# Small transfers and recurrent states begun on GpSimd's queue, and the delta sample states updated by one fp32r pass

## The chip, the cores and the metric

The kernel runs on one core of a Trainium2 chip. The metric is the device time of one execution in microseconds; lower is better. The engines are TensorE (PE, with its weight loads PEld), VectorE (DVE), ScalarE (ACT), GpSimd (POOL) and SyncE (SP, which here only issues DMAs). "SPq", "ACTq" and "POOLq" in a row are the queues of these engines: issuing a DMA is an instruction there. Sixteen DMA engines move the data.

## The reference

Two layers of a recurrent decoder run for 256 prompt tokens and 8 x 4 sample tokens (288 columns in all) with shared weights, width 2048. Cut to what matters here:

```python
# layer 0: delta-rule heads and an RG-LRU; layer 1: mLSTM heads
for layer in range(2):
    mix = delta_lru_mixer(x, ...) if layer == 0 else mlstm_mixer(x, ...)
    h = layer_norm(ALPHA * x + mix)
    h = layer_norm(ALPHA * h + square(relu(h @ w_up)) @ w_down)
    x = h + sigmoid(h @ w_ple_gate) * (p[layer] @ w_ple)

# the gated delta rule, chunk by chunk (one chunk of 4 tokens for a sample)
v_new = u_i - w_i @ s
o     = (q_i * exp(g_i)) @ s + qk_i @ v_new
s     = s * exp(g_last) + (k_i * exp(g_last - g_i)).T @ v_new     # state, 128 x 128 per head
```

The last line is done for 8 samples and 8 heads: 64 states of 128 x 128. The outputs are x and every state (conv, delta, lru, mlstm c, n, m).

## The kernel before, in words

The work of TensorE is nearly all weight products. A weight slab of 512 KB (`raw`) is loaded on SP (`convert`, L394), split by ScalarE into a high part `hi` (L294) and by VectorE into a low part `lo` (L295), and multiplied in three fp32r passes with the split activations `ah`/`al` (`tiles`, L416, 128x288 moving). Up to three slabs are prepared ahead, with four buffers.

Everything else is written as side work: Python generators (`delta_gates`, `delta_head`, `delta_sample`, `lru_block`, `mlstm_gates`, `mlstm_head`, `mlstm_sample`) that `tick` advances by one `yield` after some twelve weight matmuls. A scheduler turns the program into one instruction list for each engine, in which every instruction waits for its inputs; nothing overtakes on an engine or in its queue. DMAs that move states and small tiles are instructions in these lists too. The side matmuls have the line of the helper `mm` (L268); transposes are L272, VectorE's helpers are L255, L258 and L262, ScalarE's is L265.

The places that the change touches:

- `delta_gates` computes the gates of all heads on 8 partitions, writes them to DRAM (`dgc`, `dds`), and reloads them broadcast or regrouped (`gcb` for each head in `delta_head`, `rs`). These run on ScalarE's queue, `gcb` on SP's.
- `conv` loads the previous rows of a channel block (`sconv` into `cin`) and stores the new ones (`out_conv`) on SP.
- `delta_sample` has 8 heads by 2 groups of 4 samples (g). It loads each group of states `S` (256 KB; four buffers) for the products `m<-S,win`, with windows that GpSimd copies (L1019), solves for `y` (tile `sy`), and then loads every `S` once more for the update. For the update `y4` places the four samples of a group beside each other (128x512, zeros elsewhere), `kh` masks the keys of one head, and `m<-y,kh` is one plain fp32 matmul of 128x512 for each head and group, 16 in all. VectorE adds it to the decayed state, which SP stores.
- `mlstm_gates` does for layer 1 what `delta_gates` does for layer 0 (`mds`, `mrs`, `dw`, `w`, `dsc`, `scB`, `dng`) on ScalarE's queue; `mlstm_head` loads `ngb`, `mlstm_sample` loads and stores 16 states `cn` on SP.

```python
            y4 = lp.tile([128, 4, 128], F32, name="y4", bufs=1)
            self.tt(y4, y[:, g:g + 1].to_broadcast([128, 4, 128]),
                    c[:, C_B4:C_B4 + 4][:, :, None].to_broadcast([128, 4, 128]), ALU.mult)
```

Of the kernel before, what the change touches and what calls it, by code (L numbers as in the profile page):

```python
# [8 lines left out]
F32 = mybir.dt.float32  # L9
# [24 lines left out]
C_H8 = C_B4 + 4  # L34
C_B8 = C_H8 + 8
# [10 lines left out]
def const_table():  # L46
# [11 lines left out]
    c[:, C_B4:C_B4 + 4] = (r[:, None] // 32 == np.arange(4)[None])  # L58
    c[:, C_H8:C_H8 + 8] = ((r[:, None] % 32) // 4 == np.arange(8)[None])
# [159 lines left out]
class Trunk:  # L219
# [299 lines left out]
    def scratch(self, layer):  # L519
# [7 lines left out]
        self.nc.sync.dma_start(raw, self.t["p"][layer])  # L527
# [139 lines left out]
    def conv(self, lp, acc, c):  # L667
# [4 lines left out]
        nc.sync.dma_start(x[:, S0:], self.t["sconv"][c])  # L672
# [3 lines left out]
        nc.sync.dma_start(self.t["conv"][c], x[:, NP:])  # L676
# [20 lines left out]
    def delta_gates(self, acc, lp, T):  # L697
# [5 lines left out]
        nc.scalar.dma_start(rst, self.t["rows"][:, 0])  # L703
# [13 lines left out]
        nc.scalar.dma_start(self.dgc, gc)  # L717
# [135 lines left out]
    def delta_head(self, lp, h, kq, v, z, out):  # L853
# [3 lines left out]
        nc.sync.dma_start(gcb, self.dgc[h:h + 1].to_broadcast([128, NT]))  # L857
# [77 lines left out]
        nc.sync.dma_start(self.t["delta_p"][h], S[:, 1])  # L935
# [20 lines left out]
    def delta_sample(self, lp, win, out):  # L956
# [46 lines left out]
        X = res[0]  # L1003
        y, o = B("sy", bufs=1), B("oo")
# [3 lines left out]
        def load(h, g):  # L1008
            s = lp.tile([128, 4, 128], F32, name="S", bufs=4)
            nc.sync.dma_start(s, state(h, g))  # L1010
            return s

        for g in range(2):
# [16 lines left out]
            nc.scalar.copy(y[:, g], py)  # L1030
            yield
# [21 lines left out]
        for g in range(2):  # L1053
            y4 = lp.tile([128, 4, 128], F32, name="y4", bufs=1)
            self.tt(y4, y[:, g:g + 1].to_broadcast([128, 4, 128]),
                    c[:, C_B4:C_B4 + 4][:, :, None].to_broadcast([128, 4, 128]), ALU.mult)

            def keys(h):
                kh = lp.tile([128, 128], F32, name="kh", bufs=2)
                self.act(kh, ksc[:, g], AF.Copy, scale=c[:, C_H8 + h:C_H8 + h + 1])  # L1060
                return kh

            kh = keys(0)
            yield
            for h in range(8):
                s = load(h, g)
                pu = self.pm([128, 4, 128])
                self.mm(pu, kh, y4)
                if h < 7:
                    kh = keys(h + 1)  # L1070
                for b in range(4):
                    self.stt(s[:, b], s[:, b], self.eglS[:, h, 4 * g + b:4 * g + b + 1], pu[:, b],
                             ALU.mult, ALU.add)
                nc.sync.dma_start(self.t["delta_s"][h, :, 4 * g:4 * g + 4], s)
                yield
# [31 lines left out]
    def lru_block(self, lp, n, xr, gates, out):  # L1107
# [3 lines left out]
        nc.sync.dma_start(w, self.t["wri"][n])  # L1111
# [42 lines left out]
    def layer0_mixer(self, x, n_out):  # L1154
        nc, tc, t = self.nc, self.tc, self.t
        with ExitStack() as ctx:
# [50 lines left out]
            nc.sync.dma_start(t["lru"], self.hl)  # L1207
# [3 lines left out]
    def mlstm_gates(self, acc, lp, T):  # L1211
# [7 lines left out]
        nc.scalar.dma_start(rst, self.t["rows"][:, 1])  # L1219
        nc.scalar.dma_start(rmx, self.t["rows"][:, 2])  # L1220
# [20 lines left out]
        nc.scalar.dma_start(self.t["mm"], mo)  # L1241
        self.ts(ng, g, -1.0, ALU.mult)
        self.dng = self.dr.tile([8, NT], F32, name="dng")
        nc.scalar.dma_start(self.dng, ng)
# [8 lines left out]
        for n, r in enumerate((b4(a), mg, nm)):  # L1253
            nc.scalar.dma_start(ds[n].rearrange("b h t -> h b t"), r)
        self.rs = lp.tile([128, 3, 2], F32, name="mrs")
        for n in range(3):
            nc.scalar.dma_start(self.rs[:, n], ds[n].rearrange("(g b) h t -> (b h t) g", g=2))
        dw = self.dr.tile([8, 8, 4], F32, name="dw")
        nc.scalar.dma_start(dw, wr)
        self.w4 = lp.tile([128, 8], F32, name="w4")  # L1260
        for q in range(4):
            nc.scalar.dma_start(self.w4[32 * q:32 * q + 32], dw.rearrange("h b t -> (b t) h"))
# [3 lines left out]
        nc.scalar.dma_start(dsc, sc)  # L1266
# [285 lines left out]
```

## Time and profile before

| what | value |
|---|---|
| time, median of 3 runs | 2912.96 us (2909.19 to 2916.35) |
| profiled execution | 2916.8 us, its span 2915.0 us |
| granted clock of TensorE | 0.999 |
| TensorE busy | 2888.7 us, 99% |
| VectorE, ScalarE busy | 1732.1 us (59%), 1318.7 us (45%) |
| GpSimd busy | 57.9 us (2%), 197 instructions |
| DMA | 487.15 MB in 155298 packets, 167 GB/s in the mean |

The profile shows one execution. A time in a row is in microseconds from the start of the span; "[1.06 <-DMA S<-in_sdelta]" behind a row means that the engine was idle for 1.06 us before it and that the arrival of S ended this. The issuing of DMAs is not counted as busy time.

### The profile page before, as it was taken

The page shows a single profiled execution, that of the slowest core. Times are in us where ns is not written, and L with a number is a line of the kernel's source. Part 1 is how long each engine was busy: PE and PEld are TensorE (multiplying, and loading weights), DVE is VectorE, ACT ScalarE, POOL GpSimd, SP SyncE. Part 2 cuts the span into 40 slices and gives each one's busy share as a digit, 9 for nine tenths or more (in the row PEclk, how much of TensorE's full clock was granted, in tenths as well). Part 3 has the DMA queues.
Part 4 walks back from the last instruction along what each step waited for, and adds up shares of the span by engine and source line. Part 5 has one row for each costly group of instructions (what it writes and reads, how often), then busy time and mean ns, then how long its engine had stood idle before and what let it go on. Part 6 is the DMA issues. An engine that isn't in the chain of part 4 may idle for free.

```text
span 2915.0 us, 52851 instructions
## 1 busy us (share of the span) xinstructions
PE 2888.7 (99%) x21728; PEld 2839.1 (97%) x21728; DVE 1732.1 (59%) x2872; ACT 1318.7 (45%) x2171; POOL 57.9 (2%) x197
## 2 busy tenths in 40 slices
PE   8999999999999999999999999999999999999999
PEld 7999889999999999999999999999999999999999
DVE  7787787754454454455766666567445445445574
ACT  5555676543343343443634444436334334334362
POOL 1000100000000000000000000000000000000000
PEclk9999999999999999999999999999999999999999
DMA  6444475455555555555446665554555554555543
GB/s 225 134 127 128 151 233 174 134 191 166 167 164 164 165 167 166 162 165 166 159 157 201 198 201 172 184 167 159 166 163 163 167 167 162 165 166 166 165 156 132
DMA packets 155298, 487.15 MB, mean 167 GB/s; under 512 B 28552, under 2 KB 35888, under 8 KB 155056
## 3 DMA queue, kind: packets, MB, share of 16 engines
q1 hardware_dynamic: 151632, 483.68, 51.6%
q8 instruction: 170, 2.79, 0.4%
q10 hardware_dynamic: 3424, 0.10, 0.1%
q14 instruction: 72, 0.59, 0.1%
HBM read 466.12 MB, written 17.58 MB: 166 GB/s over the span
## 4 chain that ended last, share of the span: by engine, by line
PE 91%; DVE 5%; ACT 2%; DMA 1%; issue 1%; SPq 0%; ACTq 0%; DVEq 0%
PE acc L416 86%; PE m L268 4%; DVE Y L255 1%; DVE lo L295 1%; PE m L272 1%; ACT hi L294 1%; ACT junk L265 0%; PE m L470 0%; ACT L265 0%; DMA bh<-in_x 0%; DVE cv L258 0%; DVE al L255 0%; DVE mq L258 0%; DVE bl L255 0%; DMA S<-in_sdelta 0%
## 5 line engine op out<-in xcount | busy, mean ns | idle before, releaser
L295 DVE TENSOR_TENSOR lo<-raw,hi 128x1024 fp32r<-128x1024 f32 (+1 forms) x841 | 1027.1, 1223 | 680.6 <-ACT hi L294 679.6
L294 ACT CAST hi<-raw 128x1024 fp32r<-128x1024 f32 (+1 forms) x841 | 880.1, 1048 | 1007.3 <-PE acc L416 708.4
L416 PE MATMUL acc<-ah,hi 128*128 128x288 f32 x3328 | 998.9, 301 | 6.7 <-ACT hi L294 4.9
L416 PE MATMUL acc<-bh,hi 128*128 128x288 f32 x3328 | 989.6, 298 | 0.0
L416 PE MATMUL acc<-ah,lo 128*128 128x288 f32 x3328 | 985.1, 296 | 0.2 <-DVE lo L295 0.2
L416 PE MATMUL acc<-al,hi 128*128 128x288 f32 x3328 | 982.0, 297 | 0.9 <-DVE al L295 0.5
L416 PE MATMUL acc<-bh,lo 128*128 128x288 f32 x3328 | 981.3, 295 | 0.0
L416 PE MATMUL acc<-bl,hi 128*128 128x288 f32 x3328 | 974.1, 294 | 0.6 <-DVE bl L255 0.3
L416 PEld LDWEIGHTS acc<-ah,hi 128*128 128x128 f32 x3328 | 627.1, 189 | 12.6 <-ACT hi L294 4.9
L416 PEld LDWEIGHTS acc<-bh,hi 128*128 128x128 f32 x3328 | 624.0, 188 | 7.7 <-issue 7.1
L416 PEld LDWEIGHTS acc<-ah,lo 128*128 128x128 f32 x3328 | 627.7, 189 | 3.7 <-issue 2.3
L416 PEld LDWEIGHTS acc<-al,hi 128*128 128x128 f32 x3328 | 627.3, 189 | 3.6 <-issue 1.4
L416 PEld LDWEIGHTS acc<-bl,hi 128*128 128x128 f32 x3328 | 624.9, 188 | 1.8 <-DVE bl L255 0.8
L416 PEld LDWEIGHTS acc<-bh,lo 128*128 128x128 f32 x3328 | 625.2, 188 | 0.4
L265 ACT ACTIVATE tmp<-acc 128x288 f32<-128x288 f32 x160 | 65.8, 411 | 307.8 <-PE acc L416 307.7
L255 DVE TENSOR_TENSOR tmp<-tmp 128x288 f32<-128x288 f32 x128 | 58.8, 459 | 155.0 <-ACT tmp L265 155.0
L258 DVE SCALAR_TENSOR_TENSOR Y<-Y,acc 128x288 f32<-128x288 f32 x128 | 58.2, 455 | 112.0 <-PE acc L416 112.0
L258 DVE SCALAR_TENSOR_TENSOR cv<-cin,params,cv 128x312 f32<-128x312 f32 x96 | 51.5, 536 | 0.5
L258 DVE SCALAR_TENSOR_TENSOR cn<-cn,scB,m 128x257 f32<-128x257 f32 x64 | 27.9, 478 | 18.9 <-PE m L268 18.9
L265 ACT ACTIVATE Y<-Y,params 128x288 f32<-128x288 f32 x64 | 37.5, 633 | 0.3
L294 ACT CAST bh<-tmp 128x288 fp32r<-128x288 f32 x80 | 34.7, 434 | 6.2 <-DVE tmp L258 4.4
L258 DVE SCALAR_TENSOR_TENSOR tmp<-tmp,Z 128x288 f32<-128x288 f32 x32 | 14.6, 457 | 38.3 <-ACT tmp L265 38.3
(386 smaller groups left out, 1554.0 us busy)
## 6 DMA issues: line engine op xcount, KB each, us to landing
raw<-in_w_up SPq DMA_DIRECT2D x256, 512.0 KB
raw<-in_w_down SPq DMA_DIRECT2D x256, 512.0 KB
raw<-in_w_in_o SPq DMA_DIRECT2D x96, 512.0 KB
raw<-in_w_in_e SPq DMA_DIRECT2D x95, 512.0 KB
raw<-in_w_gate SPq DMA_DIRECT2D x64, 512.0 KB
raw<-in_w_out_e SPq DMA_DIRECT2D x32, 512.0 KB
raw<-in_w_out_o SPq DMA_DIRECT2D x32, 512.0 KB
cn<-in_smlstm SPq DMA_DIRECT2D x16, 514.0 KB
```

The lines of the kernel that those rows point to most:

```text
L255: return self.nc.vector.tensor_tensor(out=out, in0=a, in1=b, op=op)
L258: self.nc.vector.scalar_tensor_tensor(out=out, in0=a, scalar=s, in1=b, op0=op0, op1=op1)
L265: return self.nc.scalar.activation(out, a, f, **k)
L268: self.nc.tensor.matmul(out, l, r, start=start, stop=stop)
L272: self.nc.tensor.transpose(out, a, self.ident[:n, :n])
L294: self.nc.scalar.copy(hi, src)
L295: self.nc.vector.tensor_sub(lo, src, hi.bitcast(F32))
L416: self.nc.tensor.matmul(acc, l[:, k], x[r](8 * kb + k), start=at == 0, stop=at == n - 1)
```

## The change

First, nearly every DMA that isn't x, a parameter, a constant, a weight slab or the result y is issued by GpSimd (`nc.gpsimd`) and no more by SP or ScalarE. SP's instruction list goes from 1050 to 865 rows, GpSimd's from 172 to 415, and ScalarE issues no DMA any more.

Second, the keys (`ksc`) and `y` of `delta_sample` are split into a high and a low fp32r part (`parts_by_head`), each part is written to DRAM by head (`kd`, `yd`, 8 DMAs each), and reloaded so that the 128 partitions of a tile hold the four kinds of part products of two heads (4 DMAs into tiles named `kq`, 6 into tiles named `mq`). With them `m<-y,kh` is one fp32r matmul of one pass, which sums all part products; `y4` is made 8 times in place of 2. There are 16 such matmuls as before.

```diff
-        nc.sync.dma_start(x[:, S0:], self.t["sconv"][c])
+        nc.gpsimd.dma_start(x[:, S0:], self.t["sconv"][c])
...
-        nc.scalar.dma_start(self.dgc, gc)
+        nc.gpsimd.dma_start(self.dgc, gc)
...
-            nc.scalar.dma_start(self.rs[:, n], ds[n].rearrange("(g b) h t -> (b h t) g", g=2))
+            nc.gpsimd.dma_start(self.rs[:, n], ds[n].rearrange("(g b) h t -> (b h t) g", g=2))
...
-        nc.sync.dma_start(gcb, self.dgc[h:h + 1].to_broadcast([128, NT]))
+        nc.gpsimd.dma_start(gcb, self.dgc[h:h + 1].to_broadcast([128, NT]))
...
+        kd = self.parts_by_head(lp, "kd", ksc)
...
-            nc.sync.dma_start(s, state(h, g))
+            nc.gpsimd.dma_start(s, state(h, g))
...
+            if g == 1:
+                yd = self.parts_by_head(lp, "yd", y)
...
-        for g in range(2):
-            y4 = lp.tile([128, 4, 128], F32, name="y4", bufs=1)
...
-            for h in range(8):
-                s = load(h, g)
-                pu = self.pm([128, 4, 128])
-                self.mm(pu, kh, y4)
...
+        kg, yg = ([lp.tile([128, 2, 2, 128], F32, name=n) for _ in range(2)] for n in ("kq", "mq"))
+        for m in range(2):
+            for dst, src, parts in ((kg, kd, ((0, 0, 2), (64, 0, 2))), (yg, yd, ((0, 0, 1), (32, 0, 2), (96, 1, 1)))):
+                for at, first, n in parts:
+                    nc.gpsimd.dma_start(dst[m][at:at + 32 * n].rearrange("p n g d -> p n (g d)"),
+                                      src[2 * m:2 * m + 2, first:first + n].rearrange("n a b r d -> (a b r) n d"))
+        yield
+        yield
+        for m in range(4):
+            for g in range(2):
+                y4 = lp.tile([128, 4, 128], F32R, name="y4", bufs=1)
+                self.tt(y4, yg[m // 2][:, m % 2, g:g + 1].to_broadcast([128, 4, 128]),
+                        c[:, C_B4:C_B4 + 4][:, :, None].to_broadcast([128, 4, 128]), ALU.mult)
+                for i in range(2):
+                    h = 2 * m + i
+                    s = load(h, g)
+                    kh = lp.tile([128, 128], F32R, name="kh", bufs=2)
+                    self.act(kh, kg[m // 2][:, m % 2, g], AF.Copy, scale=c[:, C_H2 + i:C_H2 + i + 1])
+                    yield
+                    pu = self.pm([128, 4, 128])
+                    self.mm(pu, kh, y4)
...
+    def parts_by_head(self, lp, name, src):
+
+        dst = self.dr.tile([4, 2, 4, 8, 256], F32, name=name)
+        for n in range(2):
+            part = lp.tile([128, 2, 128], F32R, name="cm")
+            if n == 0:
+                self.nc.scalar.copy(part, src)
+                hi = part
+            else:
+                self.nc.vector.tensor_sub(part, src, hi.bitcast(F32))
+            for b in range(4):
+                self.nc.gpsimd.dma_start(dst[:, n, b],
+                                       part[32 * b:32 * b + 32].bitcast(F32).rearrange("p g d -> p (g d)"))
+        return dst
...
-            nc.scalar.dma_start(ds[n].rearrange("b h t -> h b t"), r)
+            nc.gpsimd.dma_start(ds[n].rearrange("b h t -> h b t"), r)
...
-        nc.sync.dma_start(ngb, self.dng[h:h + 1].to_broadcast([128, NT]))
+        nc.gpsimd.dma_start(ngb, self.dng[h:h + 1].to_broadcast([128, NT]))
...
-            nc.sync.dma_start(cn, self.t["smlstm"][h, :, gs])
+            nc.gpsimd.dma_start(cn, self.t["smlstm"][h, :, gs])
```

How the lists of the engines change at three places. At the start, SP's list of before has the small loads among the weight slabs of layer 0 (`raw<-in_w_in_e`):

```order
L394 DMA raw<-in_w_in_e 128x1024 x5
L672 DMA cin_140<-in_sconv 128x56
L394 DMA raw<-in_w_in_e 128x1024
L672 DMA cin_141<-in_sconv 128x56
L394 DMA raw<-in_w_in_e 128x1024 x3
L1111 DMA wri<-in_wri 128x256
L1010 DMA S<-in_sdelta 128x512
L394 DMA raw<-in_w_in_e 128x1024
L676 DMA out_conv<-cin_140 128x59
L1010 DMA S<-in_sdelta 128x512
```

GpSimd's list of the change begins with the same loads, behind two memsets and without a wait:

```order
L953 MEMSET win_144 128x480
L953 MEMSET win_145 128x480
L703 DMA bl<-in_rows 8x288
L672 DMA cin_140<-in_sconv 128x56
L672 DMA cin_141<-in_sconv 128x56
L1132 DMA wri<-in_wri 128x256
L1011 DMA S<-in_sdelta 128x512 x4
```

The loads of wri and of four S have moved from behind nine or more slabs to the first place of another queue.

At the delta gates, ScalarE's list of before has these rows (dgc, dds and rs; gcb is on SP):

```order
L717 DMA dgc<-bl 8x288 [waits DMAHW7_49,DVE_49]
L724 DMA dds<-bl 8x8x4 [waits DMAHW0_49]
L724 DMA dds<-bl 8x8x4 [waits DMAHW1_49,DVE_49]
...
L727 DMA rs<-dds 128x2x1 [waits DMAHW3_49,DMAHW0_49]
L727 DMA rs<-dds 128x2x1 [waits DMAHW5_49,DMAHW1_49]
```

GpSimd's list of the change holds all of them, with copies and convolution loads between:

```order
L717 DMA dgc<-bl 8x288 [waits DMASW7_49,DVE_49]
L724 DMA dds<-bl 8x8x4
L724 DMA dds<-bl 8x8x4 [waits DMASW1_49,DVE_49]
L861 COPY ks<-kq 128x8x4
L1020 COPY win_144<-ks 128x4x4 [waits Pool_49]
L857 DMA gcb<-dgc 128x288 [waits DMASW7_49]
L672 DMA cin_140<-in_sconv 128x56 [waits DMASW5_49,DVE_49,Activation_49]
L727 DMA rs<-dds 128x2x1 [waits DMASW0_49]
L727 DMA rs<-dds 128x2x1 [waits DMASW1_49]
```

What three queues did is now one row; gcb stands behind a copy and rs behind gcb and a load. On TensorE the first matmul that needs the solve, m<-t,cm, has 334 weight matmuls ahead in place of 332.

At the state update, TensorE's list of before has the first two update matmuls at once:

```order
L268 MATMUL m<-cv,wri 128x312
L272 MATMUL m<-consts,oo 128x128
L268 MATMUL m<-cv,wri 128x312
L268 MATMUL m<-y_5232,kh 128x512 x2
L416 MATMUL acc<-al,hi 128x288
```

GpSimd's list of the change has this for the way of y through DRAM (cm is a part of y, yd is in DRAM, mq is the reload):

```order
L1094 DMA yd<-cm 4x8x256 [waits DMASW1_49]
L1168 COPY hl<-lh 128x1 [waits DVE_49]
L1169 COPY hl<-lh 128x8
L1094 DMA yd<-cm 4x8x256 [waits DMASW2_49]
L1094 DMA yd<-cm 4x8x256 [waits DMASW3_49]
L676 DMA out_conv<-cin_141 128x59 [waits DMASW4_49,Activation_49]
L1061 DMA mq<-yd 32x2x256 [waits DMASW7_49,DMASW6_49,DMASW5_49]
L1061 DMA mq<-yd 32x2x256 [waits PE_49]
L1061 DMA mq<-yd 64x2x256 [waits DMASW2_49,DMASW3_49,DMASW1_49,DMASW0_49]
```

Eight yd issues and three of mq now lie between y and the first update matmul; that matmul has 1944 weight matmuls ahead in place of 1934, the second 1956 in place of 1934. Of the products m<-S,win, the groups behind the first stand 6 to 12 weight matmuls later (from 1759 to 1771 ahead, then from 1766 to 1777), and the last ones where they were. In layer 1 GpSimd's list has, in one row, mds, out_mm, dng, two mds, mrs, dw, dsc, two mrs, ngb, four w and scB, with two copies of v behind the first; before, all but ngb were in ScalarE's list.

## Rows read from the trace of the kernel before

**Rows 1.** The page: busy time by engine.

```profile
PE 2888.7 (99%) x21728; PEld 2839.1 (97%) x21728; DVE 1732.1 (59%) x2872; ACT 1318.7 (45%) x2171; POOL 57.9 (2%) x197
```

**Rows 2.** Waits of TensorE: engine, line, waited for; us in total, times, longest.

```profile
PE acc L416 <- ACT hi L294: 4.9, 1, 4.9
PE m L268 <- DVE t L791: 3.6, 2, 3.3
```

**Rows 3.** Timeline, TensorE, first state updates: start us, us, instruction, count.

```profile
385.14 1.02 PE L268 MATMUL m<-y,kh 128*128 128x512 f32 x2
...
386.14 0.29 PE L416 MATMUL acc<-ah,hi 128*128 128x288 f32 x1
...
387.33 0.59 PE L268 MATMUL m<-y,kh 128*128 128x512 f32 x1
```

**Rows 4.** Timeline, TensorE, fp32r side matmuls of layer 1.

```profile
1552.58 0.40 PE L268 MATMUL m<-v,k 128*128 128x258 f32 x2
1552.82 0.29 PE L416 MATMUL acc<-bh,hi 128*128 128x288 f32 x1
```

**Rows 5.** Windows: busy time by engine, granted clock, DMA share, GB/s.

```profile
core 0: us, PE busy (x) PEld busy (x) DVE busy (x) ACT busy (x) POOL busy (x), PEclk, DMA share, GB/s
...
8.00:10.00 2.00, 0.95 (x3) 0.66 (x3) 0.76 (x1) 0.91 (x2) 0.00 (x0) 1.00 1.02 415
...
28.00:30.00 2.00, 2.00 (x17) 2.00 (x16) 1.45 (x2) 1.47 (x2) 0.00 (x0) 1.00 0.00 1
```

**Rows 6.** Timeline, all engines, at the start.

```profile
0.80 0.93 POOL L953 MEMSET win<- 128x480 f32 x2
...
9.05 0.61 PE L416 MATMUL acc<-ah,hi 128*128 128x288 f32 x1 [1.74 <-ACT ah L294]
```

**Rows 7.** Timeline, SP's queue.

```profile
33.73 0.42 SPq L1010 DMA_DIRECT2D S<-in_sdelta  x1
```

**Rows 8.** Timeline, all engines, delta gates of layer 0.

```profile
48.22 0.29 ACTq L717 DMA_DIRECT2D dgc<-bl  x1
...
51.67 0.33 SPq L857 DMA_DIRECT2D gcb<-dgc  x1
...
51.92 0.91 ACTq L727 DMA_DIRECT2D rs<-dds  x2
...
55.62 0.43 DVE L255 TENSOR_TENSOR dm<-gcb,consts 128x256 f32<-128x256 f32 x1 [1.14 <-DMA gcb<-dgc]
...
58.15 0.16 DVE L255 TENSOR_TENSOR sw<-rs 128x2 f32<-128x2 f32 x1 [1.18 <-DMA rs<-dds]
...
68.19 0.63 PE L268 MATMUL m<-t,cm 128*128 128x32 f32 x4 [3.27 <-DVE t L791]
```

**Rows 9.** Timeline, GpSimd, two copies of the same size.

```profile
48.63 5.01 POOL L861 COPY ks<-kq 128x32 f32<-128x32 f32 x1 [3.28 <-DVE kq L258]
...
54.30 0.21 POOL L861 COPY ks<-kq 128x32 f32<-128x32 f32 x1 [0.40 <-DVE kq L258]
```

**Rows 10.** Timeline, SP's queue and TensorE, state products.

```profile
340.56 2.83 SPq L1010 DMA_DIRECT2D S<-in_sdelta  x4
...
345.99 0.64 PE L268 MATMUL m<-S,win 128*32 128x128 f32 x16 [1.06 <-DMA S<-in_sdelta]
```

**Rows 11.** Timeline, three engines: y complete, the first state update, one y4.

```profile
370.69 0.27 ACT L1030 COPY sy<-m 128x128 f32<-128x128 f32 x1
...
381.85 1.88 PE L268 MATMUL m<-y,kh 128*128 128x512 f32 x4
...
402.19 0.69 DVE L255 TENSOR_TENSOR y<-sy,consts 128x512 f32<-128x512 f32 x1
```

**Rows 12.** Timeline, three engines, mLSTM gates and first head of layer 1.

```profile
1533.55 0.47 POOL L1312 COPY ngs<-ngb 128x32 f32<-128x32 f32 x1 [1.61 <-DMA ngb<-dng]
...
1537.01 0.39 ACT L265 ACTIVATE D<-ngb,mtg 128x128 f32<-128x128 f32 x1
...
1538.33 1.57 PE L268 MATMUL m<-vt,sT 128*128 128x257 f32 x6 [1.45 <-DVE sT L258]
```

More of the change, by code (lines that the diff above doesn't have):

```diff
@@ L33 @@
 C_B4 = C_LEV + 128 * LEVELS
-C_H8 = C_B4 + 4
-C_B8 = C_H8 + 8
+C_H2 = C_B4 + 4
+C_B8 = C_H2 + 2
 C_VONE = C_B8 + 8
@@ L57, in const_table @@
     r = np.arange(128)
-    c[:, C_B4:C_B4 + 4] = (r[:, None] // 32 == np.arange(4)[None])
-    c[:, C_H8:C_H8 + 8] = ((r[:, None] % 32) // 4 == np.arange(8)[None])
+    c[:, C_B4:C_B4 + 4] = (r[:, None] % 32 // 8 == np.arange(4)[None])
+    c[:, C_H2:C_H2 + 2] = (r[:, None] % 8 // 4 == np.arange(2)[None])
     c[:, C_B8:C_B8 + 8] = ((r[:, None] % 32) // 4 == np.arange(8)[None])
@@ L526, in scratch @@
         raw = T("praw", [2, NT])
-        self.nc.sync.dma_start(raw, self.t["p"][layer])
+        self.nc.gpsimd.dma_start(raw, self.t["p"][layer])
         self.split(*self.php, raw)
@@ L675, in conv @@
                        acc[:, NP:].rearrange("p (b t) -> p b t", t=4))
[L676 removed]
+        nc.gpsimd.dma_start(self.t["conv"][c], x[:, NP:])
         out = lp.tile([128, S0 + 56], F32, name="cv")
@@ L702, in delta_gates @@
         x, sp, g, rst = T(), T(), T(), T()
-        nc.scalar.dma_start(rst, self.t["rows"][:, 0])
+        nc.gpsimd.dma_start(rst, self.t["rows"][:, 0])
         self.act(x, acc[0:8], AF.Identity, bias=p[0:8, P_DT:P_DT + 1])
@@ L1052, in delta_sample @@
         yield
-        for g in range(2):
-            y4 = lp.tile([128, 4, 128], F32, name="y4", bufs=1)
[L1055 to L1064, printed above, removed]
-            for h in range(8):
-                s = load(h, g)
-                pu = self.pm([128, 4, 128])
-                self.mm(pu, kh, y4)
[L1069 to L1075, printed above, removed]
+        kg, yg = ([lp.tile([128, 2, 2, 128], F32, name=n) for _ in range(2)] for n in ("kq", "mq"))
@@ new lines, in delta_sample @@
+        for m in range(2):
[19 more added lines that the diff above has]
+                    for b in range(4):
+                        self.stt(s[:, b], s[:, b], self.eglS[:, h, 4 * g + b:4 * g + b + 1], pu[:, b],
+                                 ALU.mult, ALU.add)
+                    nc.gpsimd.dma_start(self.t["delta_s"][h, :, 4 * g:4 * g + 4], s)
@@ new lines, in parts_by_head @@
+    def parts_by_head(self, lp, name, src):
[7 more added lines that the diff above has]
+                self.nc.vector.tensor_sub(part, src, hi.bitcast(F32))
+            for b in range(4):
+                self.nc.gpsimd.dma_start(dst[:, n, b],
+                                       part[32 * b:32 * b + 32].bitcast(F32).rearrange("p g d -> p (g d)"))
+        return dst
@@ L1110, in lru_block @@
         w = lp.tile([128, 2, 128], F32, name="wri")
-        nc.sync.dma_start(w, self.t["wri"][n])
+        nc.gpsimd.dma_start(w, self.t["wri"][n])
         for _ in range(2):
@@ L1206, in layer0_mixer @@
             self.finish()
-            nc.sync.dma_start(t["lru"], self.hl)
+            nc.gpsimd.dma_start(t["lru"], self.hl)
         return out
@@ L1218, in mlstm_gates @@
         ig, fg, ls, B, d1, g, m, rst, rmx, ng = (T() for _ in range(10))
-        nc.scalar.dma_start(rst, self.t["rows"][:, 1])
-        nc.scalar.dma_start(rmx, self.t["rows"][:, 2])
+        nc.gpsimd.dma_start(rst, self.t["rows"][:, 1])
+        nc.gpsimd.dma_start(rmx, self.t["rows"][:, 2])
         self.act(ig, acc[0:8], AF.Identity, bias=p[0:8, P_IG:P_IG + 1])
@@ L1379, in mlstm_head @@
         nc.scalar.copy(so, pc)
-        nc.sync.dma_start(self.t["mc_p"][h], so)
+        nc.gpsimd.dma_start(self.t["mc_p"][h], so)
         yield
@@ L1412, in mlstm_head @@
                          ALU.mult, ALU.add)
-            nc.sync.dma_start(self.t["mc_s"][h, :, gs], cn)
+            nc.gpsimd.dma_start(self.t["mc_s"][h, :, gs], cn)
     def mlstm_sample(self, lp):
```

18 lines of the change are left out of this document (9 added, 9 removed).

## The prediction

> **What bounds the kernel now.** I read the busy times first: TensorE works 2888.7 of 2915.0 us [rows 1], so all its idle time is 26.3 us. GpSimd is busy 57.9 us, VectorE 59% of the span. Then TensorE's waits: 4.9 us for the first slab at the start and 3.6 us for a transpose of the delta solve are the largest [rows 2]; none of them is for a weight slab later on. So two things can change the time: TensorE work that disappears, and the few places where a late transfer already ends, or can come to end, a wait of TensorE. The sum below is made against the profiled execution, 2916.8 us (span 2915.0 and 1.8 around it); it stands 3.8 us, 0.13%, above the median of 2912.96. What a measurement tells from no change is taken as 0.3%, 8.7 us: faster is below 2904.2, slower above 2921.7.
>
> **The saving on TensorE.** The 16 state matmuls m<-y,kh (128x512, plain fp32) are two passes each, 32 records in all. One runs from 385.14 until the weight matmul at 386.14, and one weight matmul lies between [rows 3]. Weight matmuls follow each other every 0.132 us (nine starts from 386.14 to 387.33), so one state matmul costs 1.00 - 0.13 = 0.87 us. An fp32r side matmul is in the trace too: two of 258 columns take from 1552.58 to 1552.82 [rows 4], 0.12 each, or 0.24 us for 512 columns if the time goes by columns. The saving is 16 x 0.63 = **-10.0 us**. Nearest row against it: a single half of an old state matmul shows 0.59 us, pipelined [rows 3]; if one new pass cost that, 16 x 0.28 = 4.5 us would be left. I take the fp32r row, the same kind of matmul, and keep 4.5 as the other end.
>
> **The unknown: one DMA issue on GpSimd.** 243 DMA issues come to GpSimd's queue (172 instruction rows become 415), and GpSimd issues none before, so no row has the price. From below: 0.33 us, the issue of gcb on SP [rows 8]. From above: 5.01 us, a GpSimd copy of 32 columns stretched while VectorE is at work; the same copy takes 0.21 us six microseconds later [rows 9]. Nearest in kind are S loads issued back to back on SP, 2.83 us for four [rows 10]. I take that, I = 0.7 us: these issues too write many descriptors. Each DMA queued in series ahead of one that is waited for then costs 0.35 us more than on SP or ACT. 243 x 0.7 is 170 us of GpSimd over 2915, which binds nothing by itself; what counts are five places.
>
> *Start.* Before, wri and the four first S loads stand on SP behind the first weight slabs (33.73 us, [rows 7]), where the DMA engines are free (share 0.00 in 28 to 30 us). After, GpSimd begins them with nothing ahead but two memsets. They are 4 x 262 KB + 131 KB + 2 x 29 KB = 1.24 MB, thrown among x and the first slabs, when the engines are full (share 1.02 at 415 GB/s in 8 to 10 us, [rows 5]) and TensorE waits for x (1.74 us at 9.05, [rows 6]). 1.24 MB at 415 GB/s are 3.0 us, the upper bound; zero if the ring of SP gets its bytes first. With the rows load there are eight issues of 0.7 us from 1.73 on (the end of the memsets, [rows 6]), so they end by about 7.3 us, before the wait for x at 9.05 ends, so I take **+2.5**. TensorE is the bound from there on, so the loss stays.
>
> *Delta gates.* dgc leaves at 48.22, gcb at 51.67 once dgc has landed, and dm starts on gcb at 55.62; rs is issued from 51.92 and sw waits for it until 58.15; from there VectorE runs in order to the transpose for which TensorE waits 3.27 us at 68.19 [rows 8]. After, GpSimd holds dgc, two dds, a ks copy, a win copy, gcb, a sconv load and two rs in one row. With 0.7 each dgc, dds, dds end at 50.3; the ks copy there ends at 53.6 if it is held as before (48.63 + 5.01) and at 50.5 if not; gcb is then issued by 52.4 or 54.5, the rs by 54.5 or 56.6. Landing 5.3 us after the issue as before (52.83 to 58.15) they come at 59.8 or 61.9: 1.7 or 3.7 us late. VectorE takes sw in order, so TensorE's wait grows by that, less two weight matmuls (0.27) that now stand ahead. I take **+2.5**, bounds 0 and +4.9 (I = 1.0).
>
> *State products.* The S loads before the solve go four at a time (340.56) and TensorE already waits 1.06 us for one at 345.99 [rows 10]. After, GpSimd issues 21 DMAs and 28 window copies in the 26 us of this loop: 21 x 0.7 + 28 x 0.2 = 20 us. It fits, barely; four loads come 1.4 us later, and 6 to 11 more weight matmuls stand ahead of the groups behind the first (some 1 us). I take **+1**, bounds -1.1 (the wait vanishes) and +3 (I = 1.0: 26.6 us of work in 26).
>
> *The trip through DRAM.* y is complete at 370.69 + 0.27 and the first state matmul stands at 381.85 [rows 11], after the change behind ten more weight matmuls (1.3 us), at 383.2. Between lie: the copy into high parts 0.4 us and its queue, say 371.5; eight yd issues, 5.6 us; the landing, 3.2 us (the end of dgc's issue at 48.51 to gcb's at 51.67); the last of three mq issues that wait for it, 0.7; their landing, 3.6 (gcb to dm); y4 and kh, 1.2. Together 385.8: **+2.5** late, bounds 0 (I = 0.35: 382.7) and +5.3 (I = 1.0: 388.5). kd leaves long before and waits for nobody. The six extra y4 multiplies of 0.69 us [rows 11], the VectorE subtracts and the ScalarE copies are 5 to 6 us spread over about 30 us, covered by weight matmuls; without that cover they would cost as much, but VectorE has 41% free.
>
> *mLSTM gates.* Before, ScalarE issues these DMAs itself and stands still until each source has landed, and its D starts at 1537.01 although ngb was there for GpSimd's ngs at 1533.55; TensorE waits 1.45 us for what follows [rows 12]. After, ScalarE is free, and ngb, the eleventh of a row on GpSimd, comes 10 x 0.35 = 3.5 us later, at 1537.0: an even exchange; **+0.5**, bounds -1.45 and +3.
>
> Everything else moved (out_conv, delta_s, lru, mc_s stores, cn and later gcb loads) has no TensorE wait in the list of before and is hidden by weight matmuls. Where a S load waits for a free buffer, delta_s stores and later sconv loads are queued behind it on GpSimd; their readers are convolutions further on.
>
> Sum: -10.0 + 2.5 + 2.5 + 1 + 2.5 + 0.5 = -1.0 us, 2915.8 in the profiled execution's terms, **2912.0 us** by the median. With I = 0.35 the five terms are about +1, +1, 0, 0, 0: 2905. With I = 1.0 they are +3, +4.9, +3, +5.3, +3: 2922.2.
>
> **A rule against the trace.** The stretched copy [rows 9] says that GpSimd can be held by VectorE, whose costliest instruction here, the lo subtract of raw and hi, has two SBUF inputs. The Trainium skill, "SBUF — State Buffer", section "Who interferes with whom", says that such an instruction of VectorE holds up GpSimd's reads of SBUF but not its writes, and infers that writing descriptors is spared; copies in VectorE's two-port modes would block it. By the row, issues of up to 5 us would come up, which is the third rival below; by the rule nearly none, and the sum stays. No run of before shows which.
>
> **The rivals.**
> 1. *GpSimd's issue costs 1 us or more* (slower). Place: the five places above, together; from 0.7 to 1.0 the sum grows by 10 us. It decides at I = 1.0, where the sum is 2922.2; at 1.2 it would be near 2929. For it: descriptors made by a program instead of hardware have no row yet, and each place is a chain of waits. Against it: the state products and the mLSTM gates have slack, 1 and 3.5 us, and GpSimd has next to nothing else to do. Chance 0.19.
> 2. *The small transfers land sooner on a ring of their own* (faster). Before, S loads and ngb share SP's ring with slabs of 512 KB, 1.26 us each at the 415 GB/s of [rows 5]. The waits of 1.06 for S and of 1.45 after ngb are about one slab long; without a slab ahead they vanish. With an issue of 0.4 us the start and the delta gates cost about 1 each and the DRAM trip fits: -10 + 1 + 1 - 1.06 - 1.45 = -10.5, **2902.5**. For it: all five places have a transfer on their path. Against it: rs, on ACT's ring and behind no slab, took 5.3 us all the same [rows 8]. The Trainium skill, "DMA: Bandwidth & Descriptors", section "SWDGE vs HWDGE vs iDMA", says that the two kinds of rings feed different queues inside each DMA engine, which it serves in turn; by it a small transfer would not stand behind slabs. No trace of before shows it, for GpSimd issued nothing. Chance 0.28.
> 3. *GpSimd is held by VectorE while it issues*, as the copy was [rows 9]: with one issue of 5 us in the delta gates, the DRAM trip and the mLSTM gates each, 3 x 4.3 = 13 us come on top: 2925. Chance 0.05.
> 4. *The one pass isn't cheap*, 0.59 us in place of 0.24: 16 x 0.35 = 5.6 us less saved, 2917.6. Chance 0.03.
>
> **How the numbers follow.** My forecast has 0.45, all within 0.3% but its edges; with rival 4 "same" is 0.48. Faster is rival 2, 0.28; slower rivals 1 and 3, 0.24. The range reaches from below rival 2 (2900, the start undisturbed) to a little above the point where rival 1 decides and near rival 3 (2924); it leaves out half of rival 1 and the tail of rival 2. The likeliest case's own range is 2905 to 2921.
>
> **What would show it.** In the trace of the changed kernel: m<-y,kh in 16 records with the next weight matmul about 0.25 us on; GpSimd's issues near 0.7 us; the first matmuls of 9 to 12 us moved by 2 to 3 us; the wait for the transpose t near 5.5 us in place of 3.27; a wait of about 2 us for y or kh ahead of the first state matmul; the wait at 1538 about unchanged. Wrong it would be by an issue price of 1 us or more, or 0.35; by a start that doesn't move; or if a queue on GpSimd blocks on a place that I hold for hidden, such as a S load that waits for a buffer while sconv stands behind it.

## The result, and the profile after

The changed kernel takes 2945.21 us in the median of four runs (2943.68 to 2950.49) against 2914.01 us for four runs of the kernel before, a ratio of 1.0112 (95% interval 1.0094 to 1.0131): some 31 us slower, outside the range of 2900 to 2924. The profiled execution took 2950.49 us, its span 2948.7 us.

The page of the changed kernel, busy time by engine (answers to [rows 1]), and then the largest of its waits of TensorE behind the start (to [rows 2]: us in total, times, longest; those for t, 8.1 us, and for a copy of v, 4.8 us, stand further below):

```profile
PE 2891.8 (98%) x21712; PEld 2846.9 (97%) x21712; DVE 1737.2 (59%) x2880; ACT 1320.4 (45%) x2173; POOL 188.8 (6%) x435
```

```profile
PE m L268 <- DVE y L255: 10.5, 6, 4.3
...
PE acc L416 <- DVE lo L295: 6.9, 4, 4.0
...
PE m L268 <- DMA S<-in_sdelta: 3.5, 1, 3.5
```

TensorE's idle time is 2948.7 - 2891.8 = 56.9 us in place of 26.3. Its busy time has grown by 3.1 us although 10 us of passes are gone: worked out from these two numbers, about 13 us are the same matmuls at a lower clock. The timeline shows it behind a wait: weight matmuls 0.24 us apart in place of 0.13, and the window's granted clock (the number before the DMA share) at 0.50, the lower of the two levels (1.2 of 2.4 GHz), after a window of 4 us in which TensorE worked 0.65 us. From 444.56 on the matmuls are 0.13 to 0.14 us apart again. Timeline of TensorE and two windows of the changed kernel:

```profile
440.61 0.61 PE L416 MATMUL acc<-ah,lo 128*128 128x288 f32 x1 [3.96 <-DVE lo L295]
...
441.73 0.44 PE L416 MATMUL acc<-al,hi 128*128 128x288 f32 x1
441.97 0.44 PE L416 MATMUL acc<-ah,hi 128*128 128x288 f32 x1
```

```profile
436.00:440.00 4.00, 0.65 (x2) 0.21 (x2) 2.41 (x7) 1.50 (x3) 1.35 (x3) 0.71 0.30 112
440.00:444.00 4.00, 3.40 (x14) 3.40 (x15) 3.34 (x8) 0.00 (x0) 1.62 (x3) 0.50 0.71 206
```

Where the time went can be read stage by stage, because every trace holds the same 19968 weight matmuls, in the same order but for at most 219 of them in and just behind the update. Number 600, for example, starts at 120.67 us in the trace before and at 131.53 after: up to there 10.86 us are lost. Between two such numbers the difference is a stage's loss. "Start and gates" is up to number 600, "products" 1758 to 1933 (the delta states' products), "update" 1933 to 2350, "mLSTM" 10100 to 10300; the rest is within 0.6 us everywhere, but for 1.2 us between update and mLSTM (pass only, kh and y4 on GpSimd) and 2.3 us behind mLSTM (rest on GpSimd). Losses against the profile of before, in us:

| kernel | time, median | ratio to before | start and gates | products | update | mLSTM |
|---|---|---|---|---|---|---|
| changed | 2945.21 | 1.0112 [1.0094, 1.0131] | +10.9 | +6.1 | +12.6 | +4.3 |
| pass only | 2921.43 | 1.0032 [1.0021, 1.0044] | -5.1 | +6.1 | +5.0 | +0.2 |
| queue only | 2939.94 | 1.0095 [1.0080, 1.0110] | +9.9 | +2.7 | +5.8 | +3.9 |
| gates of layer 0 back | 2935.23 | 1.0081 [1.0066, 1.0096] | -4.2 | +5.7 | +13.1 | +2.9 |
| states back | 2942.34 | 1.0103 [1.0087, 1.0119] | +8.5 | +6.0 | +4.9 | +3.8 |
| gates of layer 1 back | 2945.19 | 1.0102 [1.0085, 1.0119] | +9.6 | +5.5 | +13.4 | +0.3 |
| rest on GpSimd | 2928.59 | 1.0047 [1.0033, 1.0060] | -3.0 | +3.9 | +9.2 | +0.4 |
| pass, no trip | 2916.27 | 1.0003 [0.9994, 1.0011] | -4.0 | -0.2 | +1.3 | +0.3 |
| pass, no trip, half the additions | 2908.22 | 0.9977 [0.9967, 0.9987] | +3.2 | -0.3 | -6.2 | +0.4 |
| before, half the additions | 2909.91 | 0.9984 [0.9974, 0.9994] | -0.8 | -0.7 | -2.9 | +0.5 |
| pass, no trip, states on GpSimd | 2923.54 | 1.0024 [1.0013, 1.0034] | +2.2 | +3.6 | +1.9 | +0.5 |
| pass only, kh on GpSimd | 2927.66 | 1.0044 [1.0029, 1.0060] | -2.4 | +4.3 | +9.0 | +0.4 |
| pass only, kh and y4 on GpSimd | 2922.91 | 1.0028 [1.0018, 1.0038] | -2.8 | +5.2 | +2.2 | +0.2 |
| pass only, trip on SP | 2918.76 | 1.0018 [1.0008, 1.0028] | -4.7 | +0.1 | +6.3 | +1.1 |
| the same, kh on GpSimd | 2918.93 | 1.0015 [1.0006, 1.0025] | -4.1 | +0.3 | +5.2 | +1.0 |
| changed, eglS once | 2939.64 | 1.0090 [1.0076, 1.0104] | +0.0 | +4.9 | +11.4 | +4.0 |
| pass, no trip, a quarter off VectorE | 2912.67 | 0.9991 [0.9982, 1.0000] | -2.8 | -1.1 | -0.1 | +0.5 |
| the same, eglS once | 2912.07 | 0.9997 [0.9988, 1.0006] | -4.6 | -1.1 | +0.0 | +0.6 |

The first column of losses varies by several microseconds between executions: kernels whose start and gates are those of before stand at -5.1 to +3.2 there. The other columns repeat within one to two microseconds where nothing changed: the update of the changed kernel and of its versions with gates back stands at 12.6 to 13.4, mLSTM at 2.9 to 4.3 where its gates are on GpSimd. The median of before was 2911.27 to 2917.58 from one group of runs to another, so kernels of different groups compare by ratio.

### The profile page after: what moved, and what is told of

It is laid out like the page before. It is cut to its first block, busy times and chain, and to the rows that moved or that the text cites. A ratio compares the mean times of both kernels' runs of the same rounds, so it can differ in the third digit from the quotient of the medians.

```text
span 2948.7 us, 52917 instructions
## 1 busy us (share of the span) xinstructions
PE 2891.8 (98%) x21712; PEld 2846.9 (97%) x21712; DVE 1737.2 (59%) x2880; ACT 1320.4 (45%) x2173; POOL 188.8 (6%) x435
## 4 chain that ended last, share of the span: by engine, by line
PE 88%; DVE 4%; ACT 2%; DMA 2%; issue 1%; POOL 1%; SPq 0%; POOLq 0%; DVEq 0%; ACTq 0%
PE acc L416 84%; PE m L268 3%; DVE Y L255 1%; PE m L272 1%; DVE lo L295 1%; DMA gcb<-dgc 1%; ACT hi L294 1%; DMA out_delta_s<-S 0%; ACT L265 0%; DMA S<-in_sdelta 0%; ACT junk L265 0%; PE m L470 0%; DVE cv L258 0%; DMA bh<-in_x 0%; DVE bl L255 0%
```

## The experiments

My theory behind the result was **A**: what was three queues is one in-order row on GpSimd, and what is waited for stands there behind DMAs that wait themselves. The rival was **B**: the update itself got slower, by its trip through DRAM and the turn-round of its buffers (a state's load into a buffer, its update, and its store, until the buffer is free again).

**Pass only**: the changed kernel with all moved DMAs back on SP and ScalarE (`dgc` and `S` shown); kd, yd and their reloads stay on GpSimd.

```diff
-        nc.gpsimd.dma_start(self.dgc, gc)
+        nc.scalar.dma_start(self.dgc, gc)
...
-            nc.gpsimd.dma_start(s, state(h, g))
+            nc.sync.dma_start(s, state(h, g))
```

> The change with every moved DMA back on the queue that it had before (SP or ScalarE); only the trip of keys and y through DRAM stays on GpSimd. Theory A (the loss is the one in-order row on GpSimd: transfers that are waited for stand there behind others that wait themselves): the stages of the delta gates, the state products and the mLSTM gates take what they took before, the update stage wins 5 to 10 us; time 2904 to 2910. Theory B (the update itself is slower: the trip through DRAM and four state buffers whose turn-round now binds): the update stage still loses 8 us or more; time 2920 to 2930.

2921.43 us, +0.3%: B's time, though not its 8 us in the update. The gates come back, but the products lose 6.1 and the update 5.0 us, with no old DMA moved. Neither theory had the products.

**Queue only**: the kernel before with the other half of the change.

```diff
-        nc.sync.dma_start(gcb, self.dgc[h:h + 1].to_broadcast([128, NT]))
+        nc.gpsimd.dma_start(gcb, self.dgc[h:h + 1].to_broadcast([128, NT]))
...
```

> The kernel before with the moved DMAs on GpSimd and nothing else (the plain fp32 update stays). Theory A: delta gates +11, state products +6, mLSTM gates +4, and 0 to 8 us in the update stage; time 2934 to 2943. Theory B: the three other stages lose as in the changed kernel (some 20 us), but the update stage nothing, since its matmuls leave time for the turn-round of the buffers: 2934 at most, and without the half-speed stretches of TensorE there.

2939.94 us, within A, and the update loses 5.8 us where B had nothing; the products lose 2.7 us, not 6. So both halves lose: 0.95% the queue, 0.32% the pass; together 1.12%, a little less than their sum.

**Gates of layer 0 back** (rows, dgc, dds, rs to ScalarE; gcb to SP) and **states back** (S, delta_s to SP), each alone in the changed kernel.

```diff
-            nc.gpsimd.dma_start(self.rs[:, n], ds[n].rearrange("(g b) h t -> (b h t) g", g=2))
+            nc.scalar.dma_start(self.rs[:, n], ds[n].rearrange("(g b) h t -> (b h t) g", g=2))
...
```

> The changed kernel with only the delta gates' DMAs of layer 0 back (rows, dgc, dds, rs on ScalarE, gcb on SP). Theory A: the stage of the delta gates loses its 11.5 us wholly, the rest stays: 2933 to 2935. Rival: what is late there is the ks copy and the convolutions' loads that stay on GpSimd: less than half comes back, 2940 or more.

```diff
-                    nc.gpsimd.dma_start(self.t["delta_s"][h, :, 4 * g:4 * g + 4], s)
+                    nc.sync.dma_start(self.t["delta_s"][h, :, 4 * g:4 * g + 4], s)
...
```

> The changed kernel with only the loads of the delta states S and their stores delta_s back on SP. Theory A: state products (+6.1) and update (+12.6) both come back and the update wins its 5 to 10 us: 2918 to 2925. Theory B: the products' 6 us come back, the update stage stays about 12 us above before: 2938 to 2940.

The gates' loss goes wholly (2935.23), as A says. With the states back the update falls from +12.6 to +4.9, the level of the pass alone, while the products stay at +6.0. Neither theory had that, and 2942.34 us is above both forecasts. The time moved by only 3 us, less than the traces differ; the profiled execution of the changed kernel was its longest of four.

**Gates of layer 1 back** (all DMAs of `mlstm_gates` to ScalarE, ngb to SP).

```diff
-        nc.gpsimd.dma_start(ngb, self.dng[h:h + 1].to_broadcast([128, NT]))
+        nc.sync.dma_start(ngb, self.dng[h:h + 1].to_broadcast([128, NT]))
...
```

> The changed kernel with the mLSTM gates' DMAs and ngb back on ScalarE and SP. If TensorE's 4.8 us for a GpSimd copy of v there come from the copy standing behind these DMAs, the stage returns to within 1 us of before and the time to 2939 to 2942; else it stays at 2944 to 2947.

The stage returns to +0.3, as expected. The time doesn't show it: 2945.19 us is above the 2939 to 2942 expected, and by ratio it falls by 0.1%, which these intervals don't separate.

**Rest on GpSimd**: gates of both layers and states back, the convolutions, wri, prompt states, lru and cn stay.

```diff
-        nc.gpsimd.dma_start(self.dng, ng)
+        nc.scalar.dma_start(self.dng, ng)
...
-            nc.gpsimd.dma_start(s, state(h, g))
+            nc.sync.dma_start(s, state(h, g))
...
```

> The changed kernel with the DMAs of both gates, gcb, ngb and the delta states back on their old queues; the convolutions' loads and stores, wri, the prompt states, lru, cn and their stores stay on GpSimd. Theory A: these have slack, so the time is that of the one pass alone, 2919 to 2923. Rival: convolution loads that stand behind others on GpSimd hold up ScalarE in the first heads, 2926 or more.

2928.59 us, the rival's time; by ratio 0.15% above the pass alone, with intervals that overlap. The rival's place, the first heads, shows no loss (-3.0); the update stands at +9.2 in place of +5.0. That these transfers have slack isn't borne out there. What they hold up isn't shown.

**Pass, no trip**: the kernel before with the two tiles typed fp32r; the update's low parts are left out.

```diff
-            y4 = lp.tile([128, 4, 128], F32, name="y4", bufs=1)
+            y4 = lp.tile([128, 4, 128], F32R, name="y4", bufs=1)
...
-                kh = lp.tile([128, 128], F32, name="kh", bufs=2)
+                kh = lp.tile([128, 128], F32R, name="kh", bufs=2)
```

> The kernel before, with y4 and kh written as fp32r, so that the 16 update matmuls are one pass each; no split and no trip through DRAM (the low parts of keys and y are left out of the update), all DMAs where they were. Theory V (VectorE, 85 to 100% busy in the update stage, bounds it): TensorE's 10 us become waits for lo and S there; stage 0 to 4 us shorter, time 2908 to 2911. Theory T (the trip alone ate the gain): the stage wins 8 to 10 us, time 2901 to 2903.

This is the key run, and V a third theory. A state matmul costs 0.23 us, as worked out; timeline of TensorE in this kernel:

```profile
380.94 0.39 PE L268 MATMUL m<-y,kh 128*128 128x512 f32 x1
381.17 0.29 PE L416 MATMUL acc<-al,hi 128*128 128x288 f32 x1
```

And the time is that of before: 1.0003 [0.9994, 1.0011]. What is won at first is given back. Windows over the update, cut where weight matmuls 1933, 2066, 2210 start; first the kernel before, then this one (columns as in [rows 5]):

```profile
380.00:411.30 31.30, 30.91 (x168) 23.66 (x168) 27.73 (x83) 25.32 (x54) 0.90 (x4) 1.00 0.72 232
411.30:437.90 26.60, 25.12 (x162) 21.85 (x161) 24.90 (x60) 16.88 (x29) 1.78 (x5) 1.00 0.81 268
```

```profile
375.80:400.40 24.60, 23.21 (x154) 21.06 (x153) 22.74 (x69) 21.32 (x46) 1.57 (x4) 1.00 0.67 208
400.40:435.20 34.80, 25.67 (x158) 23.51 (x159) 28.67 (x69) 19.15 (x34) 0.79 (x3) 0.95 0.75 246
```

The first stretch is 6.7 us shorter; VectorE's share rises to 92% there and its additions fall behind. The second is 8.2 us longer: TensorE now waits for lo (6.5 us in all) and for VectorE's additions to S (2.1), and its granted clock there is 0.95 in the mean. VectorE was busy 89 and 94% of these stretches already before, where the whole span says 59%. In the second stretch of the new kernel it is busy 82%: there it stands 3.3 us for a state matmul and 2.5 us for S loads. Two of these waits in its timeline:

```profile
404.75 0.86 DVE L258 SCALAR_TENSOR_TENSOR S<-S,eglS,m 128x128 f32<-128x128 f32 x3 [3.34 <-PE m L268]
...
420.36 1.12 DVE L258 SCALAR_TENSOR_TENSOR S<-S,eglS,m 128x128 f32<-128x128 f32 x4 [1.39 <-DMA S<-in_sdelta]
```

**Half the additions**: in `delta_sample`, VectorE adds two of the four samples of a group and leaves the other states as loaded; once on the kernel with one pass and no trip, once on the kernel before.

```diff
-                for b in range(4):
+                for b in range(2):
```

> The one pass without the trip, and VectorE adds only two of the four samples of every group to the state (half of the 64 state additions, 11 us of VectorE, are left out; the low parts are left out as before). Theory V (VectorE bounds the update stage): TensorE's freed 10 us now show, the stage is 7 to 10 us shorter than before, time 2901 to 2905. Theory S (the four state buffers on SP, a load waiting for a store to land and weight slabs behind it, bound it): at most 4 us shorter, 2908 or more.

> The kernel before with the same half of the state additions left out and the plain fp32 matmuls kept. If TensorE bounds the stage there (its 76 of 80 us busy): within 3 us of before, 2909 to 2913. If VectorE does: 5 us or more faster.

With one pass, 11 us of VectorE less bring the update from +1.3 to -6.2; with the plain fp32 matmuls, from 0 to -2.9. So the additions on VectorE are most of what holds the single-pass update back, and they cost the old one some 3 us, less than the 5 that would have made VectorE its bound. Fewer additions also free the S buffers sooner; the two effects aren't separated here. The times (2908.22, 2909.91; 0.23 and 0.16% under before) go the same way, though the difference between the two is within their intervals, and neither 2901 to 2905 nor 5 us off the kernel before was reached: with half the additions ScalarE's longest wait in the stage, 4.01 us, is for a slab.

**Pass, no trip, states on GpSimd** (S and delta_s only), to see whether that list is the bound.

```diff
-            nc.sync.dma_start(s, state(h, g))
+            nc.gpsimd.dma_start(s, state(h, g))
...
```

> The one pass without the trip, with only the delta states' loads and stores on GpSimd; convolution loads and weight slabs stay on SP, where nothing waits for a state store any more. Theory S: the update stage wins 5 to 10 us, time 2902 to 2907. Theory V: within 3 us of before, 2910 to 2915.

The update stays (+1.9 for +1.3): of theory S, the part falls that SP's list, with slabs behind a state store, is the bound. The products lose 3.6 us, 1.0024, which neither theory had. That the turn-round of four buffers takes its share is left open: more than four S buffers would be the direct test, and it wasn't tried.

**kh on GpSimd**, then **kh and y4 on GpSimd**, both on the pass alone.

```diff
-                    self.act(kh, kg[m // 2][:, m % 2, g], AF.Copy, scale=c[:, C_H2 + i:C_H2 + i + 1])
+                    nc.gpsimd.tensor_scalar(out=kh, in0=kg[m // 2][:, m % 2, g], scalar1=c[:, C_H2 + i:C_H2 + i + 1], scalar2=None, op0=ALU.mult)
```

> The one pass alone (all old DMAs back on SP and ScalarE, as in the earlier experiment), and the masked keys kh made by GpSimd in place of ScalarE. If ScalarE standing 5.2 us for the reloaded keys is what costs the state products their 6 us, that stage comes to within 2 us of before and the time to 2915 to 2917. If something else in the stage is late (the kd issues ahead of the window copies), it stays at +5 or more and 2920 to 2923.

```diff
-                self.tt(y4, yg[m // 2][:, m % 2, g:g + 1].to_broadcast([128, 4, 128]), ...)
+                nc.gpsimd.tensor_tensor(out=y4, in0=yg[m // 2][:, m % 2, g:g + 1].to_broadcast([128, 4, 128]), ...)
```

> As the run with kh on GpSimd, and y4 (eight products of 128x512) on GpSimd as well, so that VectorE has 5.5 us less to do in the update stage and doesn't stand for the reload of y. Theory V: the update stage comes back by 5 to 8 us, time 2906 to 2911. Rival (the turn-round of four S buffers binds it): the stage stays at +5 over before, 2914 or more; and if GpSimd is held by VectorE's two-input work, y4 takes 3 us or more each and the stage loses.

The products stay at +4 to +5, so ScalarE's standing for keys wasn't their cause; kh on GpSimd even costs 4 us in the update, and 2927.66 us is above both forecasts. With y4 off VectorE the update goes from +9.0 to +2.2, as theory V has it, though no addition and no buffer changed; this speaks for VectorE, its work or its standing for y, against the buffers. But 2906 to 2911 was not reached, and the time is no better than that of the pass alone, whose start and gates stood 2.3 us lower.

**Trip on SP** (kd, yd and their reloads on SP, GpSimd issues nothing), and the same with **kh on GpSimd**.

```diff
-                self.nc.gpsimd.dma_start(dst[:, n, b],
+                self.nc.sync.dma_start(dst[:, n, b],
...
```

> The one pass with every DMA on its old queue and the trip through DRAM (kd, yd and their reloads) on SP as well, so that GpSimd issues nothing. If the kd issues ahead of GpSimd's window copies cost the state products their 6 us, that stage comes to within 2 us of before and the time to 2914 to 2916; if ScalarE's standing for the reloaded keys does, the stage stays at +5 or more and the time at 2919 to 2923.

> The same with kh made on GpSimd as well. If both causes add up (kd issues on GpSimd, ScalarE standing for keys), the state products come to within 1.5 us of before, which the run before doesn't reach; if the kd issues alone were it, nothing is gained over that run, and GpSimd's window copies, which now stand behind kh, make it slower.

The products' 6 us are gone (+0.1, +0.3), so the cause was the trip's issues on GpSimd; 2914 to 2916 was not reached, because the update keeps its loss. Timeline of GpSimd in the pass-only kernel, and then with the trip on SP: in the first it is idle for 12.35 us until the parts are there, issues kd for 4.82 us, and only then copies windows. The reloads of kd, which stand among these copies, moved to SP as well, and their share isn't separated.

```profile
333.54 4.82 POOL L1094 DMA_DIRECT2D kd<-cm  x8 [12.35 <-ACT cm L1089]
338.40 1.84 POOL L1020 COPY win<-ks 128x16 f32<-128x16 f32 x4
```

```profile
335.74 1.18 POOL L1020 COPY win<-ks 128x16 f32<-128x16 f32 x4 [14.16 <-PE m L268]
```

What is left is +6.3 in the update, where the same pass without the trip has +1.3. The trip's own VectorE work shows in it (72.8 us busy in that stage in place of 68.2); how much of the 5 us is that, and how much the waiting for y, isn't separated.

**eglS once**: the changed kernel, with the decays taken in one activation from GpSimd's copies `gcs`, and not head by head from gcb.

```diff
-        self.act(self.eglS[:, h], gs[:, :, 3], AF.Exp)
...
+        self.act(self.eglS.rearrange("p h (g b) -> p h g b", g=2),
+                 self.gcs[:, :, :, :, 3].rearrange("p g b h -> p h g b"), AF.Exp)
```

> The changed kernel, in which the decays eglS are made once, for all heads, from the copies gcs that GpSimd makes anyway, and not head by head by ScalarE straight from each gcb. If ScalarE standing for a gcb, with eglB and the sums of squares of the first head behind it, is a part of the 11.5 us at the delta gates (6.8 and 1.9 us of standing), that stage takes 3 to 6 us less and the time is 2939 to 2942. If only the arrival of gcb for VectorE's dm counts, the stage stays within 1.5 us.

The stage goes from +10.9 to 0.0, and the time to 2939.64, within the forecast. The times differ by 5.6 us, 0.2% by ratio, and the traces exaggerate: that of the changed kernel is its longest run, this one the shortest of its four. TensorE's wait for t goes from 8.13 to 5.24 us, and two waits of some 2 us behind it are gone; with the old queues that wait was 1.0 to 5.0 us from trace to trace, with the gates on GpSimd and eglS head by head 7.6 to 8.1. The profiles show what stood: two rows of ScalarE before, then timelines of ScalarE, VectorE and TensorE in the changed kernel:

```profile
53.73 0.16 ACT L265 ACTIVATE eglB<-m 128x16 f32<-128x16 f32 x1
...
58.01 0.20 ACT L265 ACTIVATE eglS<-gcb 128x8 f32<-128x8 f32 x1
```

```profile
58.35 0.22 ACT L265 ACTIVATE eglS<-gcb 128x8 f32<-128x8 f32 x1 [6.78 <-DMA gcb<-dgc]
58.47 0.17 ACT L265 ACTIVATE eglB<-m 128x16 f32<-128x16 f32 x1
...
58.67 0.17 DVE L255 TENSOR_TENSOR wT<-m,tg 128x16 f32<-128x16 f32 x1 [5.81 <-ACT eglB L265]
...
72.64 1.06 PE L268 MATMUL m<-t,cm 128*128 128x32 f32 x4 [8.13 <-DVE t L791]
```

The scheduler had put eglS ahead of eglB and of the sums of squares; before, eglB was done 4 us ahead of eglS. ScalarE stood for gcb with these behind it, and VectorE for them, 5.81 us for eglB and 1.95 for the sums.

**A quarter off VectorE**, the version that the runs point to, though it too leaves out the update's low parts: one pass, no trip, old queues; one sample of four is added by GpSimd from a copy that ScalarE makes. Then the same with eglS once.

```diff
...
+                        nc.scalar.copy(u, pu[:, b])
+                        nc.gpsimd.tensor_scalar(out=s[:, b], in0=s[:, b], scalar1=egl, scalar2=None, op0=ALU.mult)
+                        nc.gpsimd.tensor_tensor(out=s[:, b], in0=s[:, b], in1=u, op=ALU.add)
```

> The one pass without the trip, and for one of the four samples of a group the state addition is taken off VectorE: ScalarE copies the product out of PSUM, GpSimd scales the state and adds. VectorE has 5.4 us less to do. Theory V: the update stage is 2 to 4 us shorter than with the one pass without the trip (which took 81.1 us), time 0.1% under before. If GpSimd is held by VectorE's work, its part is late, the stores too, and the stage is as long or longer.

> The candidate that the runs point to: the old queues, one pass without the trip, a quarter of the state additions on ScalarE and GpSimd, and eglS made once. Each part takes a wait or VectorE work away: 1 to 3 us under the run without the last part, ratio 0.997 to 0.999 to before. If the single-pass gain is out of reach as long as VectorE and the state buffers bind the stage, it stays at 0.999 to 1.000.

0.9991 and 0.9997: better than the changed kernel by more than 1%, but not shown to be better than before. The update is 1.4 us shorter than with all additions on VectorE, less than the 2 to 4 expected and hardly clear of what the column varies by; eglS once adds nothing on the old queues.

## Why the prediction was wrong, point by point

Forecast and measured, term by term: start +2.5 and -0.7; delta gates +2.5 and +11.5; products +1 and +6.1; saving and trip together -7.5 and +12.6; mLSTM gates +0.5 and +4.3.

- *"The saving is 16 x 0.63 = -10.0 us"*. The price of the matmul held (0.23 us for 0.24), the step from it to the time failed, and with it "VectorE has 41% free". That is the mean of the span. In the first two thirds of the update VectorE was 89 to 94% busy, and TensorE's 10 us became waits, most of them for VectorE's lo and S. The pass without the trip gained nothing (1.0003), and gains once VectorE has less to do. With the price rival 4 falls.
- *I = 0.7 us* for an issue was too high: 32 S loads on GpSimd took 0.536 us at least, 0.542 in the median, 0.600 at most, below the value taken. The row that it was taken from was misread: the four loads on SP in 2.83 us [rows 10] are issues of 0.33 to 0.37 us with waits between them. So rival 1 had the right side by a wrong mechanism. Its place was right, its price not: what costs is not the issue but who stands behind it. Rival 3 falls with the same numbers. By the rule of the Trainium skill ("SBUF — State Buffer", "Who interferes with whom") a VectorE instruction with two SBUF inputs doesn't hold up a GpSimd instruction that only writes SBUF; from this the Trainium skill infers that descriptor writing is spared. The trace agrees: issues that overlap a lo subtract took 0.03 us more than the others of their kind at most, and none over 0.76 us, while a ks copy took 3.40 us.
- *Delta gates*: gcb left at 52.70, rs by 55.29, both within or ahead of the times worked out, and the wait came out at 8.13 us for 3.27 [rows 8]. The failed step is that only DMAs were followed. The new order on ScalarE, where eglS stands for gcb ahead of eglB, was not costed. By the times this order is somewhat more than half of the stage's loss: eglS once takes 5.6 us off the changed kernel, the gates' DMAs on their old queues 10.0. What is left shows at gcb: with eglS once VectorE's dm still waits 4.90 us for it, 1.14 before [rows 8].
- *State products* "+1": the window copies were counted, but not that kd stands ahead of them on GpSimd and waits for ScalarE. "kd leaves long before and waits for nobody" was the wrong step. In the changed kernel TensorE's wait for S is 3.54 us for 1.06 [rows 10]. In the pass-only kernel the trip put on SP takes the loss away; the S loads on GpSimd cost 2.7 and 3.6 us of their own where there is no trip (queue only; pass, no trip, states on GpSimd), and in the changed kernel the two don't add up.
- *The trip* "+2.5": TensorE waited 1.87 us for y at the first update matmul, near the forecast. What was missed is later: the five other waits for y, 8.6 us, and S loads that stand on GpSimd until a store has landed, 23.0 us in all. The prediction held this place for hidden and named it as a sign of being wrong; with the states back on SP the update's loss falls by 7.7 us.

```profile
L1011 POOL DMA_DIRECT2D S<-in_sdelta x32 | 17.4, 546 | 29.1 <-DMA out_delta_s<-S 23.0 <-PE m L272 2.9 <-DVE S L258 2.7
```

  How much of the +12.6 each moved group has is not settled: the runs with the trip lie between +2.2 and +13.4, and with each move the scheduler reorders the rest. Argued, not shown: the spread is these orders.
- *mLSTM gates* "+0.5": ngb was followed, the copies of v behind it were not. Row by row in GpSimd's timeline of the changed kernel, with TensorE's wait at the end:

```profile
1563.73 0.75 POOL L1278 DMA_DIRECT2D mrs<-mds  x1 [2.23 <-DMA mds<-al]
...
1568.62 0.29 POOL L1338 COPY v<-mv 128x128 f32<-128x128 f32 x1
...
1568.97 0.47 PE L272 MATMUL m<-consts,v 128*128 128x128 f32 x1 [4.78 <-POOL v L1338]
```

- *Start* "+2.5": no loss is seen beside the scatter, which is -2.9 to +2.8 us at weight matmul 200 with the old queues. The wait for x at [rows 6] was 0.96 us in place of 1.74, with 1.24 MB more in flight.
- Rival 2, transfers that land sooner on their own ring, isn't seen: gcb took 5.05 us from the end of its issue (53.30) to ScalarE's eglS at 58.35; before, 3.6 us from the end of its issue (52.00) to dm [rows 8].
- No term had the clock: beside waits of 2.1 to 8.1 us TensorE ran stretches at the lower level, 0.50, which cost some 13 us in all, as worked out above; a wait of 2.2 us at 425.15 had none.

## What to carry to other kernels

Read the busy shares in the stage that a change touches: work taken from the engine that ends the span was worth nothing here, where another engine was about 90% busy behind it. Before a DMA is moved to another queue, list what stands behind it there, computing instructions too, and what it waits for itself; an issue of half a microsecond was cheap here, an in-order row that stands for a landing was not. And look at the new order of every engine that reads what is moved, since a scheduler may put the first reader ahead of work that was ready.

## What the runs showed of the hardware

A DMA issue on GpSimd occupied it for 0.54 us (S, 256 KB) to 0.76 us (mrs), without stretching beside VectorE; on SP the S issues took 0.35 us in the median. Small GpSimd copies took 0.2 to 3.4 us in the changed kernel, and up to 5.0 in the kernel before. The plain fp32 matmul of 128x512 cost 0.87 us and the fp32r one 0.23. Beside most waits of 2 to 8 us TensorE ran some microseconds with weight matmuls 0.24 us apart, at a granted clock of 0.50: with 30.6 us more of waits came some 13 us more of slow matmuls.
